# Copies of the weights back to DRAM, spread over four passes by their place in the tile instead of three passes by piece number

## The chip, the cores and the metric

The kernel runs on all 8 cores of one Trainium2 chip. Each core works on its own sequences; the weights are the same for all, and no core waits for another. The metric is the device time of the slowest of the 8 cores in one execution, in microseconds (us). As the slowest of eight is noisy, I also use the mean span of the 8 cores over all fast runs ("mean of the cores").

Some executions fall in a slow state: the cores of one die, sometimes of both, have a lower mean granted TensorE clock (0.81 to 0.97), and the execution takes 2217 to 2540 us. They are left out everywhere, so all medians below are of the fast runs alone.

## The reference, cut to what matters

```python
xn = rmsnorm(x, g_pre_mix)
z  = xn @ w_in                         # xa, ga, u, v, gates: six projections of 1024
# A: conv -> gates -> scan -> * gelu(ga) -> @ w_br_a      (merge piece "ba")
# B: gelu(u) * (w_s @ layernorm(gelu(v)) + b_s) -> @ w_br_b   (merge piece "bb")
mix = (sigmoid(g_a) * o_a + sigmoid(g_b) * o_b) @ w_out   # "ma", "mb", "out"
x = x + rmsnorm(mix)
gate, up = split(rmsnorm(x) @ w_ffn_in)                   # "fg", "fu"
x = x + rmsnorm((silu(gate) * up) @ w_ffn_out)            # "fo": the channel mixer
```

The inputs are float32; the kernel multiplies in bf16.

## The kernel before

A core has nine tiles of at most 512 tokens. The weights are not kept on chip: every tile streams all of them through a ring of 8 slots, in 70 pieces, nearly all of 128 x 2048 elements. The projections have 16 pieces (xa, v, ga, u), the merge 20 (mb, bb, ma, ba, out), the channel mixer 34 (fg, fu, fo).

A piece is first read as f32 from `wall` by a DMA that GpSimd issues and that casts to bf16. In one chosen pass (0 for tile 0, 1 for tile 1 and so on) the bf16 piece is copied back from the ring to a DRAM scratch `wsc`. From then on SyncE loads it as bf16 from there: half the bytes to read.

```python
def PASS_OF(pid):
    return pid % 3

def load(pid):
    slot = free.popleft()
    have[pid].append(slot)
    n = PIECES[pid][2] * PIECES[pid][4]
    if pid in cached:
        dma("sp", ... wring[:, slot, 0:n] <- wsc[pid, :, 0:n] ...)
        return
    dma("pool", ... wring[:, slot, 0:n] <- wall[pid, :, 0:n] ...)
    k = seen.get(pid, 0)
    seen[pid] = k + 1
    if k == PASS_OF(pid):
        todo_wo[slot] = (pid, n)        # to be copied back when it has landed

def copy_back(slot):
    pid, n = todo_wo.pop(slot)
    dma("sp", ... wsc[pid, :, 0:n] <- wring[:, slot, 0:n] ...)
    cached.add(pid)
```

The order of instructions is not written by hand. The work is cut into stages ("v of tile 1, rows 0 to 127", "second norm of tile 0, part 3"). A list scheduler on the host keeps a clock for every engine and for DMA, and always emits the stage that can start earliest, by priority among those ready. A dry run fixes the order in which pieces are streamed; the second run records the program. The DMA clock charges by kilobytes, so it sees f32 loads as twice as long:

```python
DMA_NS, DMA_LAT = 3.3, 2000.0
...
self.dma_free = max(self.dma_free, start) + kb * self.DMA_NS
...
while True:
    fill()                                  # copies and loads that may go now
    best = None
    for e in P.ENGS:
        on = [(offer(q[0]), rank(q[0], n), q) for n, q in streams.items() if ...]
        ...
    if best is None:
        break
    emit(best[1][2].popleft())
...
plan = record(Prog(), None)                 # dry run
P = Prog()
record(P, plan)
```

Of the kernel before, what the change touches and what calls it, by code (L numbers as in the profile page):

```python
# [32 lines left out]
def piece_table():  # L33

    tab = []
    ids = {}

    def add(name, items):
        ids[name] = []
        for it in items:  # L40
            ids[name].append(len(tab))
            tab.append(it)

    add("xa", [("w_in", 0, 8, 256 * h, 256) for h in range(4)])
    add("v", [("w_in", 4 * kh, 4, 3 * D + 512 * n, 512) for n in range(2) for kh in range(2)])
    add("ga", [("w_in", 0, 8, D + 256 * h, 256) for h in range(4)])
    add("u", [("w_in", 0, 8, 2 * D + 256 * h, 256) for h in range(4)])
    add("mb", [("w_in", 0, 8, 5 * D + 256 * h, 256) for h in range(4)])
    add("bb", [("w_br_b", 0, 8, 256 * h, 256) for h in range(4)])
    add("ma", [("w_in", 0, 8, 4 * D + 256 * h, 256) for h in range(4)])  # L50
    add("ba", [("w_br_a", 0, 8, 256 * h, 256) for h in range(4)])
    add("out", [("w_out", 4 * kh, 4, 512 * n, 512) for n in range(2) for kh in range(2)])
    add("fg", [("w_ffn_in", 0, 8, 256 * q, 256) for q in range(NFF // 2)])
    add("fu", [("w_ffn_in", 0, 8, DFF + 256 * q, 256) for q in range(NFF // 2)])
    add("fo", [("w_ffn_out", 4 * r, 4 if r < 5 else 2, 512 * n, 512) for n in range(2) for r in range(6)])
    return tab, ids


PIECES, PID = piece_table()


def PASS_OF(pid):

    return pid % 3
NPIECE = len(PIECES)


class _Op:
# [213 lines left out]
def build_program():  # L282
    nc = bass.Bass("TRN2", target_bir_lowering=False)

    def din(name, shape):
        return nc.dram_tensor(name, list(shape), F32, kind="ExternalInput").ap()
# [7 lines left out]
    sc_in = din("sc", [128, NCH, 2, 3])  # L294
    wall = din("wall", [NPIECE, 128, PSZ])
    vecs_in = din("vecs", [128, NVEC, NCH])
# [12 lines left out]

    wsc = nc.dram_tensor("wsc", [NPIECE, 128, PSZ], BF16).ap()  # L310

# [3 lines left out]
    with contextlib.ExitStack() as es:  # L315
# [79 lines left out]
        def record(P, plan):  # L395
# [71 lines left out]
            cached = set()  # L467
            have = {pid: deque() for pid in range(NPIECE)}
            todo_wo = {}
            wo = deque()  # L470
# [6 lines that stand above are left out]
                    dma("sp", lambda e: e.dma_start(out=wring[:, slot, 0:n], in_=wsc[pid, :, 0:n]), ring_sems[slot], n / 4,  # L477
                        [("wsc", pid)], [("wr", slot)])
                    return
                dma("pool", lambda e: e.dma_start(out=wring[:, slot, 0:n], in_=wall[pid, :, 0:n]), cast_sems[slot], n / 2,  # L480
                    (), [("wr", slot)])
# [3 lines that stand above are left out]
                    todo_wo[slot] = (pid, n)  # L485
# [934 lines left out]
def make_in_maps(inputs):  # L1420
    f = lambda a: np.ascontiguousarray(np.asarray(a, dtype=np.float32))
    g = {k: f(v) for k, v in inputs.items()}
    wall = np.zeros((NPIECE, 128, PSZ), np.float32)
    for i, (name, k0, kc, c0, n) in enumerate(PIECES):
# [39 lines left out]
```

## Time and profile before

| | |
|---|---|
| time, median | 2179.73 us |
| mean of the cores (9 fast runs, on the chip of experiments 1 to 4) | 2170.5 us |
| f32 loads / bf16 loads / copies back | 139 / 491 / 70 |

The page of the slowest core. Part 1 gives busy time and share by engine, part 2 shares in 40 slices of the span (tenths), part 3 the DMA queues (q1: SyncE's plain transfers; q0: GpSimd's casting loads), part 4 the chain of waits that ended last.

```profile
span 2202.9 us, 34614 instructions; the slowest of 8 cores (2163.8 to 2202.9 us)
PE 2086.7 (95%) x10518; PEld 1021.6 (46%) x10666; DVE 1203.0 (55%) x1880; ACT 901.9 (41%) x1536; POOL 380.2 (17%) x761
...
DMA  9698899987778657773545554576575666365663
...
q1 hardware_dynamic: 97362, 341.48, 46.4%
q0 software_dynamic: 20016, 72.36, 20.8%
...
PE 85%; DMA 6%; DVE 3%; issue 3%; ACT 3%; POOL 1%; SPq 0%; DVEq 0%; POOLq 0%; ACTq 0%
```

(148 matmul records of this core are missing from the trace: 10666 weight loads, 10518 matmuls.) PE is the limit, and DMA is close to full (8 or 9 tenths in eight of the first nine slices) only in the first fifth of the span, while most pieces still come as f32. From part 3, 139 f32 loads take 20.8% of 16 engines' 2202.9 us, 3.3 us of all 16 for each; the plain queue takes 1.57 us per 512 KB.

Spans and clocks of four cores:

```profile
core 0: 2169.2 us, clock 0.981
...
core 3: 2163.8 us, clock 0.983
core 4: 2202.9 us, clock 0.970
core 5: 2192.6 us, clock 0.970
```

Cores 4 and 5 of this execution were held at clock 0.81 from about 552 us on, for 142 and 161 us. The other six cores ran the same program without that (0.97 to 1.00 at 560 to 690 us), so I read stages on core 0. Stretches of core 0: each line has the stretch, its length, busy us (and instructions) of PE, PEld, DVE, ACT, POOL, the granted clock, the DMA share, GB/s.

```profile
core 0: us, PE busy (x) PEld busy (x) DVE busy (x) ACT busy (x) POOL busy (x), PEclk, DMA share, GB/s
0.00:250.00 250.00, 198.51 (x908) 91.34 (x909) 167.83 (x250) 148.55 (x224) 72.95 (x146) 0.90 0.86 178
250.00:350.00 100.00, 100.00 (x463) 45.23 (x462) 32.46 (x48) 14.56 (x25) 13.90 (x27) 1.00 0.93 175
425.00:450.00 25.00, 19.15 (x78) 7.90 (x78) 15.62 (x23) 10.32 (x18) 5.70 (x16) 0.86 0.91 256
480.00:550.00 70.00, 62.58 (x312) 29.08 (x311) 58.28 (x89) 44.41 (x67) 17.57 (x38) 0.95 0.77 177
550.00:660.00 110.00, 110.00 (x530) 50.54 (x528) 36.58 (x55) 22.84 (x45) 12.80 (x26) 1.00 0.92 203
```

The matmul count is the number to read. A full 25 us holds some 116 matmuls of 512 columns (0.216 us each); narrower ones take less (8 of 128 columns took 0.45 us on core 0 of before at 396 us), so a full stretch can hold more. At 425 to 450 us there are 78: a hole in tile 1's merge. At 480 to 550 us tile 1 goes from its merge to its channel mixer.

### The profile page before, as it was taken

The numbers are of one execution on the slowest core, as the hardware profiler recorded it, in microseconds if no ns is written. First come the engines' busy times: TensorE is split into PE (matmuls) and PEld (weight loads), VectorE is DVE, ScalarE is ACT, GpSimd is POOL, SyncE is SP. The second block draws the span as 40 slices with busy tenths as digits, with TensorE's granted clock in tenths as the row PEclk, the third lists the DMA queues.
The fourth block names the chain that finished last, engine by engine and source line by source line (L and its number), as shares of the span: only waits on it lengthen the run. The fifth ranks groups of instructions, "written<-read, shape, count | busy, mean of one in ns | idle before, by whom it ended". The sixth has DMA issues, their size and how long they took to land.

```text
span 2202.9 us, 34614 instructions; the slowest of 8 cores (2163.8 to 2202.9 us)
## 1 busy us (share of the span) xinstructions
PE 2086.7 (95%) x10518; PEld 1021.6 (46%) x10666; DVE 1203.0 (55%) x1880; ACT 901.9 (41%) x1536; POOL 380.2 (17%) x761
## 2 busy tenths in 40 slices
PE   4899799998999999999999999999999999899998
PEld 2344344444444444444444444455555645445553
DVE  5757634468322685167833585268357636763342
ACT  3737511465112571147412571266148224722211
POOL 2213212322002220022001210121022012112000
PEclk8899899999888999999999999999999999999999
DMA  9698899987778657773545554576575666365663
GB/s 187 141 196 164 166 185 200 254 202 172 170 178 221 191 188 185 209 240 131 182 149 188 199 191 150 170 246 220 191 256 182 224 188 231 122 201 173 200 203 108
DMA packets 117703, 416.10 MB, mean 189 GB/s; under 512 B 14537, under 2 KB 14545, under 8 KB 117522
## 3 DMA queue, kind: packets, MB, share of 16 engines
q1 hardware_dynamic: 97362, 341.48, 46.4%
q0 software_dynamic: 20016, 72.36, 20.8%
q8 instruction: 90, 1.47, 0.3%
q14 instruction: 91, 0.75, 0.1%
q10 hardware_dynamic: 144, 0.05, 0.0%
HBM read 432.62 MB, written 53.54 MB: 221 GB/s over the span
## 4 chain that ended last, share of the span: by engine, by line
PE 85%; DMA 6%; DVE 3%; issue 3%; ACT 3%; POOL 1%; SPq 0%; DVEq 0%; POOLq 0%; ACTq 0%
PE ps L707 58%; PE ps L1236 13%; PE ps L1140 5%; PE ps L954 5%; DMA wring<-wsc 2%; DMA wring<-wall 2%; DMA xin<-xp 1%; PE ps L659 1%; DVE xcf L830 1%; PE ps L848 1%; PE ps L1249 1%; PE ps L1016 1%; DMA x<-xp 0%; ACT ffT L653 0%; POOL stats L638 0%
## 5 line engine op out<-in xcount | busy, mean ns | idle before, releaser
L707 PE MATMUL ps<-hnT,wring 128*128 128x512 bf16 (+2 forms) x3133 | 637.6, 364 | 8.6 <-DVE hnT L664 4.1
L707 PE MATMUL ps<-xnT,wring 128*128 128x512 bf16 (+2 forms) x2842 | 615.9, 366 | 21.3 <-DMA wring<-wall 7.2
L707 PEld LDWEIGHTS ps<-hnT,wring 128*128 128x128 bf16 x3168 | 311.8, 99 | 325.3 <-issue 56.1
L707 PEld LDWEIGHTS ps<-xnT,wring 128*128 128x128 bf16 x2880 | 281.0, 99 | 303.8 <-issue 59.7
L1236 PE MATMUL ps<-wring,ffT 128*128 128x512 bf16 (+1 forms) x1334 | 303.8, 387 | 3.6 <-DVE hnT L664 1.7
L1215 ACT ACTIVATE sgt<-ps 128x512 f32<-128x512 f32 (+2 forms) x198 | 109.5, 554 | 448.7 <-PE ps L707 419.2
L1219 DVE SCALAR_TENSOR_TENSOR sgt<-sgt,ps 128x512 f32<-128x512 f32 (+2 forms) x198 | 125.4, 633 | 234.9 <-PE ps L707 230.8
L1236 PEld LDWEIGHTS ps<-wring,ffT 128*128 128x128 bf16 (+1 forms) x1364 | 134.5, 99 | 170.6 <-issue 34.6
L830 DVE SCALAR_TENSOR_TENSOR xcf<-xa,vecs_sb,xcf 128x512 f32<-128x512 f32 (+2 forms) x240 | 163.5, 681 | 26.8 <-DVE xcf L830 1.2
L480 POOL DMA_DIRECT2D wring<-wall x139 | 78.9, 568 | 461.9 <-PE ps L707 305.2
L1104 DVE SCALAR_TENSOR_TENSOR ffT<-ffT,ps 128x512 f32<-128x512 f32 (+1 forms) x122 | 76.3, 631 | 149.2 <-PE ps L707 130.0
L1221 DVE SCALAR_TENSOR_TENSOR ffT<-sgt,ps 128x512 bf16<-128x512 f32 (+2 forms) x198 | 125.8, 635 | 46.4 <-PE ps L707 43.0
L1095 ACT ACTIVATE ffT<-ps 128x512 f32<-128x512 f32 (+1 forms) x128 | 69.1, 554 | 164.2 <-PE ps L707 153.3
L707 PE MATMUL ps<-gsT,wring 128*128 128x512 bf16 (+2 forms) x569 | 127.4, 367 | 4.2 <-DVE gsT L1036 2.8
L707 PE MATMUL ps<-hgT,wring 128*128 128x512 bf16 (+2 forms) x568 | 124.8, 363 | 5.5 <-ACT ffT L1095 5.1
L631 POOL TENSOR_SCALAR stats<-stats 128x1 f32<-128x1 f32 (+1 forms) x132 | 34.9, 264 | 539.7 <-ACT ffT L644 442.4
L1140 PE MATMUL ps<-wring,vnm 128*128 128x512 bf16 (+1 forms) x517 | 117.1, 383 | 7.8 <-POOL vnm L1110 3.1
L954 PE MATMUL ps<-wring,xnT 128*128 128x512 bf16 (+1 forms) x513 | 116.1, 379 | 1.6 <-DMA wring<-wsc 0.8
L1259 ACT ACTIVATE sgt<-ps 128x512 f32<-128x512 f32 x66 | 38.5, 594 | 175.1 <-PE ps L1236 159.0
L638 POOL TENSOR_TENSOR stats<-stats,nhalf 128x1 f32<-128x1 f32 x165 | 100.0, 606 | 24.5 <-POOL stats L631 0.5
L1110 POOL TENSOR_TENSOR vnm<-ffT 128x512 bf16<-128x512 f32 (+1 forms) x58 | 69.2, 1194 | 191.5 <-DVE ffT L1104 143.6
L887 DVE TENSOR_TENSOR_SCAN chI<-chA,hst,chI 128x512 f32<-128x512 f32 (+1 forms) x72 | 89.1, 1237 | 7.8 <-DVE chI L886 0.5
(141 smaller groups left out, 1962.6 us busy)
## 6 DMA issues: line engine op xcount, KB each, us to landing
wring<-wsc SPq DMA_DIRECT2D x475, 512.0 KB, 4.6
wring<-wall POOLq DMA_DIRECT2D x137, 512.0 KB, 9.3
wsc<-wring SPq DMA_DIRECT2D x68, 512.0 KB, 8.6
xin<-xp SPq DMA_DIRECT2D x30, 512.0 KB, 7.4
x<-xp SPq DMA_DIRECT2D x29, 512.0 KB, 8.3
yp<-x SPq DMA_DIRECT2D x29, 512.0 KB, 6.9
wring<-wsc SPq DMA_DIRECT2D x16, 256.0 KB, 3.6
yp<-xin SPq DMA_DIRECT2D x4, 256.0 KB, 2.0
```

Source lines behind the costliest of these rows:

```text
L480: dma("pool", lambda e: e.dma_start(out=wring[:, slot, 0:n], in_=wall[pid, :, 0:n]), cast_sems[slot], n / 2, (), [("wr", slot)])
L638: pool(lambda e: e.tensor_tensor(out=stats[0:PT, r2:r2 + 1], in0=stats[0:PT, r:r + 1], in1=nhalf[0:PT, :], op=ALU.pow), 180, [("st", r), ( ...
L707: mm(lambda e, k=k: e.matmul(ps[:, b, 0:nt], lhsT=wv[:, k, m * 128:(m + 1) * 128], rhs=rhsT[:, k, 0:nt], start=(k == 0), stop=(k == NCH - ...
L830: dve(lambda e, k=k, dst=dst, win=win: e.scalar_tensor_tensor(out=dst, in0=win(k), scalar=vecs[:, V_CW + k, c:c + 1], in1=dst, op0=ALU.mul ...
L887: dve(lambda e: e.tensor_tensor_scan(out=chI[:, j, 0:np_], data0=chA[:, j, 0:np_], data1=chI[:, j, 0:np_], initial=hst[:, c:c + 1], op0=AL ...
L954: mm(lambda e, k=k, wv=wv, b=b: e.matmul(ps[0:PT, b, :], lhsT=xnT[:, k, col:col + PT], rhs=wv[:, k % 4, :], start=(k == 0), stop=(k == NCH ...
L1104: dve(lambda e: e.scalar_tensor_tensor(out=ap[:, 0:nt], in0=tsg[i][0][:, 0:nt], scalar=1.0, in1=ps[:, b, 0:nt], op0=ALU.add, op1=ALU.mult) ...
L1140: mm(lambda e, k=k, n=n, wv=wv: e.matmul(ps[0:PT, pr + n, :], lhsT=mixT[:, k, col:col + PT], rhs=wv[:, k % 4, :], start=(k == 0), stop=(k ...
L1215: act(lambda e: e.activation(out=sgt[:, i, 0:nt], in_=ps[:, b, 0:nt], func=AF.Tanh, scale=0.5), nt, [("ps", b)], [("sgt", i)])
L1219: dve(lambda e: e.scalar_tensor_tensor(out=sgt[:, i, 0:nt], in0=sgt[:, i, 0:nt], scalar=1.0, in1=ps[:, bg, 0:nt], op0=ALU.add, op1=ALU.mul ...
L1221: dve(lambda e: e.scalar_tensor_tensor(out=ffT[:, j, 0:nt], in0=sgt[:, i, 0:nt], scalar=0.5, in1=ps[:, bu, 0:nt], op0=ALU.mult, op1=ALU.mu ...
L1236: mm(lambda e, j=j, kk=kk, b=b, PT=PT, col=col: e.matmul(ps[0:PT, b, :], lhsT=ffT[:, j, col:col + PT], rhs=wv[:, kk, :], start=(j == 0), s ...
```

## The change

The intent is to take copies out of the first tile's channel mixer, where DMA is close to full (share 0.93 at 250 to 350 us), and to spread them by what the piece is used for: projections in passes 1 and 2, merge in 1 to 3, channel mixer in 2 to 4 (counted from 1).

```diff
 PIECES, PID = piece_table()
+NPIECE = len(PIECES)
 
 def PASS_OF(pid):
 
-    return pid % 3
-NPIECE = len(PIECES)
+    kind = next(k for k, v in PID.items() if pid in v)
+    i = PID[kind].index(pid)
+    if kind in ("xa", "v", "ga", "u"):
+        return i % 2
+    return i % 3 + (1 if kind in ("fg", "fu", "fo") else 0)
```

## The prediction

> **What bounds it now.** PE. On the page of the slowest core (core 4, 2202.9 us) PE is busy 95% and holds 85% of the chain of waits; DMA holds 6%. Core 4 is slowest by its clock: about 0.8 from 550 to 700 us, where core 3 (2163.8 us) has 1.00. DMA matters early: its share is 0.9 to 1.0 up to 450 us, then 0.4 to 0.8. Most other idle time of PE up to 550 us is startup and dependent work. DMA clearly costs one hole: the chain shows two bf16 loads of 17.7 and 15.3 us at 411-446 us, in tile 1's merge; cores 0, 3, 4 run 78, 83, 89 matmuls at 425-450 instead of 117: 6 to 8 us lost.
>
> **Costs.** By the queue table, 139 f32 loads take 20.8% of 16 engines' span, 3.3 us each; the plain queue takes 46.4% for 341 MB, 1.6 us per 512 KB: a bf16 load or a copy. An f32 load in place of a bf16 one adds 1.7 us. [...]
>
> **What changes.** Counting pieces: f32 loads 139 -> 159 (by pass 70/46/23/0 -> 70/52/27/10); copies 70 (24/23/23/0 -> 18/25/17/10). DMA time +35 us. By place:
> - Tile 0 before its channel mixer, with tile 1's first projections: copies 12 -> 18 of pass 1, +3 of pass 2: +13 us DMA in 0-250 us, where its share is 0.8 to 0.9. Estimate +3 us.
> - Tile 0's channel mixer (250-350 us, DMA 0.95 to 1.0, PE full): 12 copies go, -19 us DMA. The ring enters tile 1 full.
> - Tile 1's v and merge, with tile 2's first projections (350-500): about 8 f32 loads and 5 copies fewer, -22 us DMA. The hole goes: -7 us.
> - Tile 1's channel mixer: f32 loads 22 -> 34, copies 11 -> 12, +22 us DMA where its share is 0.9 (cores 0, 3). Like tile 0's before: saturated, PE full, ring drained at the end. +1 us.
> - Tiles 2 and 3: channel mixers with 22 and 10 f32 loads at shares of 0.7 to 0.8: hidden.
>
> Sum -3 us. The host's list scheduler models DMA too, so instruction order shifts: +-8 us, and more for throttling.
>
> **Predicted: 2177 us, 8 in 10 between 2150 and 2200. Faster by over 2%: 0.03; within 2%: 0.94; slower by over 2%: 0.03.**
>
> **What would show it.** 159 f32 loads, 70 copies; no long bf16-load steps in the chain at 400-450 us, about 117 matmuls per 25 us there on unthrottled cores; DMA share of 250-350 us down to about 0.85, of 550-660 us up to about 1.0 with PE still full; PE waits for f32 loads before 250 us up a few us. The clock's dip to 0.86 beside the hole goes [...].
>
> **What would make it wrong.** Tile 1's channel mixer (about 128 us of DMA against 113 us of matmuls) stalling PE: +10 to 20 us. The first 250 us being tighter than their share says, since copies wait for their f32 load at the head of the queue that also issues bf16 loads (SP waited 227 us so). Or the hole being queue order, not bandwidth, and only moving.

Two passages that no run of this case shows are cut from this text. No term of its sum goes with them: +3 -7 +1 = -3 us stands in full. But its "DMA time +35 us" adds f32 loads, bf16 loads and copies, and that these add up on the same 16 engines was the author's assumption: the page charges both queues to 16 engines (46.4% and 20.8% of their span in the kernel before), and no run tests it.

## More of the kernel before

PE's waits on core 0 from 390 to 620 us (waiting line, releaser: us in total, times, longest):

```profile
PE ps L707 <- DMA wring<-wsc: 5.6, 2, 4.8
PE ps L1016 <- DVE vnm L990: 4.7, 2, 3.3
PE ps L707 <- ACT gvf L967: 1.9, 1, 1.9
```

`wring<-wsc` is a bf16 load (the hole). L1016 is the spatial matmul of tile 2, which waits for the layernorm of v just before it.

## The result, and the profile after

| | before | after |
|---|---|---|
| time, median | 2179.73 us (3 fast of 4 runs) | 2169.02 us (2166.51 to 2171.38, 4 runs) |
| ratio of fast runs | | 0.9947, 95% interval 0.9928 to 0.9967 |
| the same, another chip, 5 rounds | 2181.00 us | 2165.69 us; 0.9923 (0.9901 to 0.9945) |
| mean of the cores, that other chip | 2170.5 us | 2153.2 us |

A ratio is the mean time of one kernel's fast runs over that of the other's fast runs of the same rounds, so it is not quite the ratio of the medians. The gain is clear of noise and below 2%.

The page of the slowest core after:

```profile
span 2169.8 us, 34771 instructions; the slowest of 8 cores (2141.6 to 2169.8 us)
PE 2068.7 (95%) x10666; PEld 1014.1 (47%) x10666; DVE 1204.7 (56%) x1880; ACT 902.4 (42%) x1537; POOL 393.2 (18%) x781
...
DMA  8799798877999498855776454656575676365563
...
q1 hardware_dynamic: 94482, 332.56, 46.2%
q0 software_dynamic: 22896, 81.27, 23.4%
...
PE 83%; DMA 7%; DVE 4%; issue 2%; ACT 2%; POOL 1%; DVEq 0%; POOLq 0%; SPq 0%; ACTq 0%
```

The same four cores after, none at a low clock for long:

```profile
core 0: 2145.6 us, clock 0.988
...
core 3: 2163.9 us, clock 0.986
core 4: 2141.6 us, clock 0.987
core 5: 2151.8 us, clock 0.988
```

There are now 159 f32 loads, 471 bf16 loads and still 70 copies. DMA works more, not less: the two queues' shares times the span are 1480 us before and 1510 us after. Yet the program is faster. The same stretches of core 0 after:

```profile
core 0: us, PE busy (x) PEld busy (x) DVE busy (x) ACT busy (x) POOL busy (x), PEclk, DMA share, GB/s
0.00:250.00 250.00, 202.68 (x942) 92.49 (x943) 165.25 (x241) 151.32 (x228) 70.69 (x143) 0.93 0.87 190
250.00:350.00 100.00, 95.50 (x467) 43.97 (x465) 55.41 (x86) 19.59 (x33) 19.61 (x40) 1.00 0.90 156
425.00:450.00 25.00, 23.48 (x109) 10.40 (x108) 22.30 (x32) 18.79 (x30) 6.85 (x15) 1.00 0.88 211
480.00:550.00 70.00, 70.00 (x373) 33.67 (x372) 58.08 (x87) 38.52 (x59) 18.52 (x37) 1.00 0.90 191
550.00:660.00 110.00, 110.00 (x535) 50.86 (x534) 39.90 (x55) 25.89 (x49) 20.26 (x39) 1.00 0.99 219
```

The hole at 425 us is nearly gone (78 to 109 matmuls). But the largest step is at 480 to 550 us: 312 to 373. Of PE's waits on core 0 from 390 to 620 us one line is left:

```profile
PE ps L711 <- DMA wring<-wsc: 1.5, 1, 1.5
```

(All lines moved down by 4; L711 was L707.) The layernorm wait of tile 2 is gone, although copies do not touch it. The reason is the order: the order of matmuls on PE differs from that of before in many places, from tile 0's v on. In the changed kernel tile 1's v runs at about 234 to 274 us, from the end of tile 0's merge into the first matmuls of its channel mixer; before, it came at about 345 to 359 us, after that mixer's gate and up matmuls. So the change did two things at once, and the trace alone cannot say which counts.

**A measure of lost PE time.** On a core whose trace has all 10666 matmul records, each record can be matched with its stage, since the program's order is known. I take the start-to-start time of successive matmuls beyond 0.216 us (or beyond the shortest seen at that place on any core, where that is less), and sum it by the tile of the later matmul. Below are means over the complete cores, in us; before is without core 5, which was at clock 0.81. The rest of the time is the same work at full clock; the 11 us before the first matmul are not counted.

| | tile 0 and startup | tile 1 | tile 2 | tiles 3 to 8 | sum |
|---|---|---|---|---|---|
| before | 59.6 | 9.1 | 16.7 | 42.9 | 128.4 |
| after (the run after_again below) | 54.3 | 13.8 | 4.6 | 40.8 | 113.4 |

The sum falls by 15.0 us, the mean of the cores by 17.3 us. All but some 2 us of it is in tiles 0 to 2. As a yardstick of noise: the first profile of the changed kernel, on the other chip, gives 54.9 / 12.4 / 4.4 / 42.8, sum 114.5. So two profiles of one program differ by up to 2 us in a column, and a difference of that size is not to be relied on.

### The profile page after: what moved, and what is told of

It is laid out like the page before. It is cut to its first block, busy times and chain, and to the rows that moved or that the text cites. A ratio compares the mean times of both kernels' runs of the same rounds, so it can differ in the third digit from the quotient of the medians.

```text
span 2169.8 us, 34771 instructions; the slowest of 8 cores (2141.6 to 2169.8 us)
## 1 busy us (share of the span) xinstructions
PE 2068.7 (95%) x10666; PEld 1014.1 (47%) x10666; DVE 1204.7 (56%) x1880; ACT 902.4 (42%) x1537; POOL 393.2 (18%) x781
## 4 chain that ended last, share of the span: by engine, by line
PE 83%; DMA 7%; DVE 4%; issue 2%; ACT 2%; POOL 1%; DVEq 0%; POOLq 0%; SPq 0%; ACTq 0%
PE ps L711 56%; PE ps L1240 13%; PE ps L1144 5%; DMA wring<-wall 4%; PE ps L958 4%; DMA xin<-xp 2%; DVE xcf L834 1%; PE ps L663 1%; PE ps L852 1%; PE ps L1253 1%; PE ps L1020 1%; ACT ffT L657 0%; POOL stats L642 0%; DVE ffT L1108 0%; DVE xcf L830 0%
## 5 line engine op out<-in xcount | busy, mean ns | idle before, releaser
L711 PE MATMUL ps<-hnT,wring 128*128 128x512 bf16 (+2 forms) x3168 | 628.5, 359 | 8.3 <-DMA wring<-wall 6.0
L711 PE MATMUL ps<-xnT,wring 128*128 128x512 bf16 (+2 forms) x2880 | 610.5, 363 | 16.0 <-DMA wring<-wall 8.6
L711 PEld LDWEIGHTS ps<-hnT,wring 128*128 128x128 bf16 x3168 | 308.2, 98 | 317.8 <-issue 16.4
L711 PEld LDWEIGHTS ps<-xnT,wring 128*128 128x128 bf16 x2880 | 279.2, 99 | 294.6 <-issue 39.5
L1240 PE MATMUL ps<-wring,ffT 128*128 128x512 bf16 (+1 forms) x1364 | 297.4, 379 | 1.7 <-DVE hnT L668 1.5
L484 POOL DMA_DIRECT2D wring<-wall x159 | 89.3, 563 | 495.7 <-PE ps L711 357.7
L711 PE MATMUL ps<-hgT,wring 128*128 128x512 bf16 (+2 forms) x576 | 125.6, 362 | 6.9 <-ACT ffT L1099 6.7
L711 PE MATMUL ps<-gsT,wring 128*128 128x512 bf16 (+2 forms) x576 | 125.3, 362 | 3.9 <-DVE gsT L1040 2.9
L958 PE MATMUL ps<-wring,xnT 128*128 128x512 bf16 (+1 forms) x528 | 121.3, 385 | 6.2 <-DMA wring<-wall 5.7
L1271 DVE TENSOR_TENSOR gvf<-ps,gbc_pf 128x512 f32<-128x512 f32 (+1 forms) x33 | 20.6, 684 | 145.5 <-ACT sgt L1263 145.5
```

The costliest lines, as they stand in the source:

```text
L484: dma("pool", lambda e: e.dma_start(out=wring[:, slot, 0:n], in_=wall[pid, :, 0:n]), cast_sems[slot], n / 2, (), [("wr", slot)])
L711: mm(lambda e, k=k: e.matmul(ps[:, b, 0:nt], lhsT=wv[:, k, m * 128:(m + 1) * 128], rhs=rhsT[:, k, 0:nt], start=(k == 0), stop=(k == NCH - ...
L958: mm(lambda e, k=k, wv=wv, b=b: e.matmul(ps[0:PT, b, :], lhsT=xnT[:, k, col:col + PT], rhs=wv[:, k % 4, :], start=(k == 0), stop=(k == NCH ...
L1240: mm(lambda e, j=j, kk=kk, b=b, PT=PT, col=col: e.matmul(ps[0:PT, b, :], lhsT=ffT[:, j, col:col + PT], rhs=wv[:, kk, :], start=(j == 0), s ...
```

## The experiments

Theory "copies": the time comes from the moved DMA work, as predicted. Theory "order": it comes from the other order that the scheduler settles on. To part them, the scheduler first plans under one rule, then its order of stages and its choice of PSUM banks (the buffers that matmuls write) are replayed while copies and loads follow another rule. The order in which pieces are streamed into the ring stays that of the plan, so here it counts as part of the order. The core of that edit, cut:

```diff
-        def record(P, plan):
+        def record(P, plan, pass_of, forced=None):
...
-                if k == PASS_OF(pid):
+                if k == pass_of(pid):
...
+            for key in forced[0] if forced else ():
+                fill()
+                assert home[key][0].key == key
+                emit(home[key].popleft())
-            while True:
+            while not forced:
...
-        plan = record(Prog(), None)
+        plan = record(Prog(), None, ORDER_PASS)[0]
+        _, order, picks = record(Prog(), plan, ORDER_PASS)
         P = Prog()
-        record(P, plan)
+        record(P, plan, COPY_PASS, (order, picks))
```

With both rules alike the replay gives the program of before, and that of after, stage for stage on every engine. All twelve runs gave correct results; each call had 5 rounds with the kernel before on the same chip.

### 1. old_order_new_copies

`ORDER_PASS = by_number` (pid % 3), `COPY_PASS = by_place` (the change).

> The order of stages on every compute engine and the choice of PSUM banks are those of the kernel before (planned with the old rule and then replayed); only the passes in which pieces are copied back, and so which loads are f32 or bf16, are those of the change. Theory 'order' (the 12 us come from the different order that the host's planner settled on): within 4 us of before, about 2177 to 2185 us, and PE still loses matmuls at 480 to 550 us (about 310 instead of 325 or more per 70 us on undisturbed cores). Theory 'copies' (the 12 us come from the lighter DMA load at 350 to 500 us, as predicted): about 2170 us, ratio 0.995 or below, and at 425 to 450 us about 117 matmuls per core instead of about 80.

Measured: 2188.64 us median, ratio 1.003 (1.0011 to 1.0048); mean of the cores 2174.9 against 2170.5 us. The new copies alone make the kernel slower. Stretches of core 0, columns as above, and its longest PE wait from 390 to 620 us (L1044 was L1016):

```profile
425.00:450.00 25.00, 24.39 (x114) 10.78 (x112) 16.80 (x25) 12.65 (x23) 6.04 (x15) 1.00 1.02 272
480.00:550.00 70.00, 61.62 (x301) 28.44 (x299) 56.90 (x86) 42.70 (x65) 19.09 (x38) 0.95 0.64 156
```

```profile
PE ps L1044 <- DVE vnm L1018: 5.5, 2, 4.0
```

The hole is gone (114 matmuls), as theory "copies" said, and the gap at 480 to 550 us stays (301), as theory "order" said. Both mechanisms are real. Its lost time is 67.6 / 9.4 / 13.1 us in tiles 0, 1, 2: a cost of 8.0 us in tile 0 outweighs a gain of 3.3 in tiles 1 and 2.

### 2. new_order_old_copies

The reverse.

> The reverse: order of stages and PSUM banks are those of the changed kernel, the passes of the copies those of before (pid % 3; 139 f32 loads). Theory 'order': keeps most of the gain, 2168 to 2173 us, with 350 or more matmuls at 480 to 550 us. Theory 'copies': loses it, about 2181 us, ratio 1.00, with a hole of 6 to 8 us again in tile 1's merge at 400 to 450 us.

Measured: 2176.97 us median, ratio 0.9994 (0.9969 to 1.0019); mean of the cores 2162.5 us, 8.0 below before. So the slowest core shows no clear gain, the mean of the cores does. The same stretches of core 0, and below them its longest PE waits from 390 to 620 us (lines moved down by 28: L735 was L707, L1168 was L1140):

```profile
425.00:450.00 25.00, 19.82 (x77) 8.13 (x76) 12.77 (x19) 8.91 (x16) 5.14 (x16) 0.84 1.02 269
480.00:550.00 70.00, 62.64 (x299) 28.42 (x300) 51.25 (x77) 44.64 (x68) 15.64 (x32) 0.95 0.73 188
```

```profile
PE ps L735 <- DMA wring<-wsc: 5.2, 1, 5.2
PE ps L1168 <- DMA wring<-wall: 4.8, 2, 3.4
PE ps L735 <- DMA wring<-wall: 1.7, 1, 1.7
```

The hole is back (77). And at 480 to 550 us the new order is no better than the old one (299): the layernorm wait is gone, but PE now waits there for f32 loads (`wring<-wall`), which the old copies still ask for. My expectation of 350 or more matmuls was a miss. Of these four kernels only the one with both changes fills this stretch: 312 before, 301 and 299 with one change, 373 with both. As such a count also depends on how many narrow matmuls fall into the stretch, here is the lost time between 480 and 550 us too, mean of the complete cores: 10.0 us before, 9.7 and 7.3 with one change, 1.0 with both (after_again).

### 3. number_plus_one

```diff
-    return pid % 3
+    return (pid + 1) % 3
```

> The kernel before with (pid + 1) % 3 in place of pid % 3, planned freely: as many copies in each pass but for one, DMA work equal to one f32 load, another arrangement. Theory 'order' (the planner's result moves by several us with any change of the rule): away from before by 4 us or more in either direction. Theory 'copies': within 3 us of before, since the DMA work by stage is the same.

Measured: 2192.06 us, ratio 1.0033 (0.9999 to 1.0066); mean of the cores 2172.9 against 2170.5 us. The ratio is not clear of noise. By the mean of the cores kernel and before differ by 2.4 us, which is within the 3 us of theory "copies", by the medians by 11 us, which is theory "order"; so the time decides nothing. Below the surface the order did move: lost time is 48.4 / 25.9 / 14.0 us in tiles 0, 1, 2 against 59.6 / 9.1 / 16.7 before. Shifts of over 10 us per tile came out nearly even.

### 4. after_again

The changed kernel once more, beside the three above.

> The changed kernel itself again, on the same chip as the three others and interleaved with the kernel before: ratio 0.994 to 0.996 under either theory. If it is nearer to 1, the gain is smaller than first measured.

Measured: 2165.69 us, ratio 0.9923; mean of the cores 2153.2 us. The four corners, by the mean of the cores, all from one chip:

| | old copies | new copies | effect of the copies |
|---|---|---|---|
| old order | 2170.5 | 2174.9 | +4.4 |
| new order | 2162.5 | 2153.2 | -9.3 |
| effect of the order | -8.0 | -21.7 | |

The gain of 17.3 us is not a sum of two parts. The new copies pay only in an order that suits them.

### 5 and 6. new_order_mixer_moved, new_order_rest_moved

New order; only the channel mixer's copies by place (172 f32 loads), or only those of projections and merge (126). Against the replay with both rules by place:

```diff
-COPY_PASS = by_place
+COPY_PASS = mixer_by_place      # fg, fu, fo by place, the others pid % 3
...
-COPY_PASS = by_place
+COPY_PASS = rest_by_place       # fg, fu, fo pid % 3, the others by place
```

> Order of stages and banks of the changed kernel, replayed; only the channel mixer's copies go by place (passes 2 to 4), projections and merge by number as before; 172 f32 loads. The gap to close is the 1.3 per cent between the new order with old copies (mean of all cores 2162.5 us) and the changed kernel (2153.2 us). If what helps is that tile 0's channel mixer no longer copies back, this closes most of it: mean of the cores 2151 to 2156 us, ratio 0.992 to 0.995, and tile 0 before its channel mixer loses no more than with the old copies. If what helps is the fewer f32 loads of projections and merge in pass 2, it stays at 2160 to 2165 us, ratio 0.998 to 1.001, with PE waiting for bf16 loads again at 425 to 455 us.

> The complement: order of the changed kernel, only projections and merge by place, the channel mixer by number; 126 f32 loads, 30 copies in pass 1. If the relief of tile 0's channel mixer is what helps: mean of the cores 2160 to 2168 us, ratio 0.998 to 1.003, since tile 0 has the extra copies and the mixer keeps its own. If the lighter pass 2 of projections and merge is what helps: 2153 to 2157 us, ratio 0.993 to 0.996.

Measured: mixer moved 2168.62 us, ratio 0.9936 (0.991 to 0.9961), mean of the cores 2157.4, between the two ranges that I had named; rest moved 2164.71 us, ratio 0.9915 (0.989 to 0.9941), mean 2152.6. The kernel before, on that chip: mean 2170.2. Emptying the first channel mixer of copies gives about half of what the copies are worth (5.1 of 9.3 us by the mean of the cores); the fewer f32 loads of projections and merge give all of it, with the mixer's copies left where they were. The mixer's part of the change adds nothing on top (2153.2 for all, in run 4).

### 7 and 8. after_v_late, before_v_early

Is tile 1's v, moved in front of tile 0's channel mixer, the piece of the order that matters? One more constraint for the scheduler, in each direction:

```diff
 # changed kernel: tile 1's v waits for the last gate and up matmuls of tile 0
-after=[("xte", t, s)] + ...
+after=[("xte", t, s)] + ([("fin", 0, NFF - 1)] if t == 1 else []) + ...
 # kernel before: tile 0's channel mixer waits for tile 1's v
-after=[("hte", t, ns - 1)] + ...
+after=[("hte", t, ns - 1)] + ([("v", 1, 3)] if t == 0 and j == 0 else []) + ...
```

> The changed kernel, planned freely, but tile 1's projection v must come after the last gate and up matmuls of tile 0's channel mixer, about where it stood in the kernel before. If v's place in front of the channel mixer (where the new order has it fill the wait for tile 0's second norm) is what the order is worth: tile 0's wait for its transposes comes back, some 10 us at 225 to 250 us, and the mean of the cores rises by 5 us or more to 2158 us or above, ratio 0.996 or above. If other parts of the order are worth more: below 2156 us, ratio up to 0.994.

> The reverse on the kernel before: tile 1's v is forced ahead of tile 0's channel mixer, the rest planned freely, copies by number. If v's place is the cause: tile 0's wait for the second norm shrinks from 10 us to under 4 us and the mean of the cores falls from 2170 to 2163 us or below, ratio 0.997 or below. The planner's own model says the opposite (slower), since the rest of the order moves too; if that holds: ratio 1.00 or above, and v's place alone is not the cause.

Measured: v late 2164.14 us, ratio 0.9917 (0.9889 to 0.9946), mean of the cores 2152.9, as fast as the changed kernel. v early 2192.49 us, ratio 1.0033 (1.0002 to 1.0064), mean 2178.6, slower than before. This piece of the order is not the cause; for v early the scheduler's own clock had said so in advance. The wait for tile 0's second norm does follow v (5.1 us with v late, none in the changed kernel, 4.4 with v early, 10.5 before), but the time comes back elsewhere: v late loses 57.4 / 9.0 / 5.6 us in tiles 0, 1, 2, v early 48.9 / 38.2 / 8.1.

### 9. before_v2_early

The kernel before, with the layernorm wait of tile 2 attacked directly:

```diff
-after=[("hte", t, ns - 1)] + ...
+after=[("hte", t, ns - 1)] + ([("v", 2, 3)] if t == 1 and j == 2 else []) + ...
```

> The kernel before, copies by number, with one more rule for the planner: tile 2's v must be done before the third gate matmul group of tile 1's channel mixer. Up to 500 us the order is unchanged. In the kernel before, the spatial matmuls of tile 2 come straight after the last of v and wait 3.3 and 1.4 us for its layernorm (5.0 us lost at tile 2's sp, mean of the complete cores). If that piece of the order is what the new order saves at 480 to 560 us: the loss at tile 2's sp falls under 1 us and the mean of the cores falls by 4 to 6 us, ratio 0.997 to 0.998. If the loss only moves to the next stage: within 2 us of before.

Measured: 2184.62 us, ratio 0.997 (0.9919 to 1.002), inconclusive by time. On the chip of runs 9 to 12 five of the nine fast runs of before were disturbed (means of the cores of 2175.6 to 2180.0, the others 2169.0 to 2170.8), so I compare with 2170: this kernel's mean is 2170.2. PE waits of core 1 from 480 to 620 us:

```profile
PE ps L707 <- DMA wring<-wall: 4.9, 1, 4.9
PE ps L707 <- ACT gvf L967: 1.9, 1, 1.9
PE ps L659 <- ACT ffT L653: 0.8, 2, 0.4
```

The loss at tile 2's spatial stage fell from 5.0 to 0.1 us, and one of 4.9 us for an f32 load took its place on core 1. Tile 2 as a whole loses 9.7 us (16.7 before), tile 1 loses 17.0 (9.1 before). The loss moved; this is the second part of what I had expected.

### 10 and 11. new_order_proj_moved, new_order_merge_moved

New order; only the projections' copies by place (132 f32 loads), or only the merge's (133), all others by number.

> Order of the changed kernel, replayed; only the projections' copies by place, merge and channel mixer by number; 132 f32 loads. Copies of pass 1 rise by 2, f32 loads of projections in pass 2 fall from 10 to 8, in pass 3 from 5 to 0. Of the 10 us (mean of the cores, 2162.5 against 2152.6) that projections and merge are worth together, the projections' share is estimated at 4 to 6 us: 2157 to 2159 us, ratio 0.994 to 0.996.

> The same with only the merge's copies by place; 133 f32 loads. Copies of pass 1 rise by 4, f32 loads of the merge in pass 2 fall from 14 to 10. If the merge's f32 loads make the hole in tile 1's merge, this takes the larger part: 2153 to 2157 us, and the loss at 425 to 455 us falls from 5.6 to about 2 us. Tile 0 before its channel mixer loses 4 to 6 us more than with the old copies (42 us).

Measured, by the mean of the cores: 2157.4 (projections; 2175.34 us median, ratio 0.9929, 0.9885 to 0.9973) and 2153.4 (merge; 2166.65 us, ratio 0.9894, 0.9833 to 0.9954). The ratios share the disturbed runs of before and look too good. Lost time with the new order and different copies:

| copies by place | tile 0 | tile 1 | tile 2 | tiles 0 to 2 |
|---|---|---|---|---|
| none (new_order_old_copies) | 50.0 | 26.7 | 7.7 | 84.4 |
| projections | 56.0 | 18.0 | 1.4 | 75.4 |
| merge | 50.3 | 20.2 | 6.9 | 77.4 |
| channel mixer | 49.6 | 19.0 | 5.9 | 74.5 |
| projections and merge | 55.9 | 13.2 | 3.1 | 72.2 |
| all (after_again) | 54.3 | 13.8 | 4.6 | 72.7 |

Each part alone saves 7 to 10 us, two or three together only 12, which suggests that they relieve the same backlog of the ring in tiles 1 and 2. The order of the rows is not to be read: in tiles 3 to 8, where little differs, these six profiles lose 37.5 to 43.5 us, and by the mean of the cores the merge's copies alone (2153.4) beat the projections' alone (2157.4). Nor does the stretch at 480 to 550 us decide the time. On core 1 the projections' copies fill it and the merge's do not, first line and second:

```profile
480.00:550.00 70.00, 70.00 (x367) 33.48 (x366) 58.23 (x88) 41.32 (x63) 16.96 (x33) 1.00 0.73 183
480.00:550.00 70.00, 65.78 (x327) 30.20 (x326) 53.89 (x82) 42.08 (x65) 18.68 (x36) 0.98 0.72 178
```

The guess about the merge's loads and the hole was wrong: with the merge moved, the loss at tile 2's first projection, where the hole sits in this order, is still 5.3 us (5.6 with none moved); with the projections moved it is 0.0, but 6.0 us appear in tile 1's merge. The extra cost in tile 0 comes with the projections' copies (50 to 56 us), not with the merge's (50.3), though I had expected it of the merge's.

### 12. v_late_rest_moved

The version that the runs pointed to: order planned by the new rule with v late, replayed with projections and merge by place and the mixer by number (126 f32 loads).

> The best version that the runs so far point to: the order planned by the new rule with tile 1's v held behind tile 0's channel mixer (tiles 0 to 2 lost 66 us there against 67 in the changed kernel, with less in tile 1), replayed with the lighter copies (projections and merge by place, channel mixer by number, 126 f32 loads). If the two add up: mean of the cores 2149 to 2152 us, ratio 0.990. If v late needs the ring that the moved mixer copies leave: slower than the changed kernel, ratio 0.994 or above.

Measured: 2164.47 us (2162.5 to 2172.36), ratio 0.9891 (0.9851 to 0.9931) against a disturbed before; mean of the cores 2150.8 us, 2.4 below the changed kernel's 2153.2 on another chip. Lost time is 57.8 / 9.1 / 3.0 us. The mean is in the range expected if the two add up. But the two kernels were never run side by side: the changed kernel has means of 2153.5 and 2153.2 us on its two chips, and the undisturbed runs of before have 2170.0 to 2170.5 on three. So a small gain is likely and not shown.

## Why the prediction was right or wrong

- **The time.** Predicted 2177 us (2150 to 2200, within 2% at 0.94); measured 2169.02, and 2165.69 on another chip. Range and class are right. The sum of -3 us was too small: -11 and -15 us by the medians. That its sign came out right was luck: in the order that the sum took as given, the same copies cost 4.4 us (run 1).
- **PE-bound, and DMA-limited only early: right.** PE stays at 95%, and all but some 2 us of the saved PE idle time lies in tiles 0 to 2.
- **Counts: right.** 159 f32 loads, 70 copies, HBM reads up by 8.9 MB, DMA time up by 30 us (predicted 35).
- **"The hole goes: -7 us": right, isolated by run 1.** With the old order and the new copies, 78 matmuls at 425 to 450 us become 114, and the losses of tile 2's two stages around the hole fall from 8.2 to 2.2 us, so -6.0. The sign I had named for it was wrong in one point: a bf16 load of 15 us still stands in the chain of waits at 423 to 438 us after the change, but PE waits only 1.5 us for it. A long transfer in the chain is not a long wait. As predicted, the clock at 425 to 450 us rises from 0.86 to 1.00: before, core 0 was granted clock 0.50 for 6.8 us from 442.2 us on, 2.3 us into its wait of 4.8 us for a load. The dip went with the hole on core 0 of all four kernels: 0.86 and 0.84 where the hole is (before, run 2), 1.00 and 1.00 where it is gone or nearly so (run 1, after).
- **"Tile 0: +3 us": right in sign, too small.** Lost time in tile 0 rises by 8.0 us in the old order and by 4.3 in the new one. The sign named for it came, larger than "a few us": PE's waits for f32 loads before 250 us rise from 5.3 to 14.5 us on core 0. I took the DMA share of 0.86 for free room. But that is an average: in run 1, 6.6 us of the cost stand at tile 0's v (0.1 before), where PE of core 0 waits 3.8 us for an f32 load; the DMA share there is 0.93 at 60 to 80 us and 0.31 at 80 to 100 us (0.83 and 0.34 before). That copies hold this load up is likely, not shown.
- **"Tile 1's channel mixer saturated, PE full: +1 us": right.** DMA share 0.92 to 0.99, PE busy 110.00 of 110 us both times.
- **DMA share of 250 to 350 us "down to about 0.85": right for the copies** (0.93 to 0.80 in run 1), but 0.90 in the changed kernel, where the new order puts tile 1's v there.
- **"Instruction order shifts: +-8 us": the step that failed.** I took the order for noise, centred on zero and independent of the copies. It is neither: in the new order the kernel is 8.0 us faster with old copies and 21.7 us faster with new ones, by the mean of the cores (with old copies the slowest core shows no clear gain, ratio 0.9994). The copies' own effect, which I put at -3, is +4.4 in the old order and -9.3 in the new. A likely reason, not tested: the scheduler charges f32 loads twice and chooses an order in which that DMA load can be borne, so rule and order belong together.
- **What stays open.** Which stages of the order carry the gain. Two candidates were tried (tile 1's v, tile 2's v), and both only moved the loss. Shown is the place where the two meet: at 480 to 550 us PE is full only with the new order (which removes the layernorm wait) and the new copies (those of the projections are enough there; they remove the waits for f32 loads). Even that place is not the whole gain: with only the merge's copies moved it is not full, and the mean of the cores is as good (2153.4). That the planner's tie of rule and order explains all 17 us is argued, not shown.

All 159 f32 loads of the changed kernel are in GpSimd's queue and all 471 bf16 loads in SyncE's. Whether the casting loads could be issued elsewhere was not tested.

## What to carry to other kernels

When a host-side scheduler models the resource you change, a change of data movement is also a change of instruction order: budget the order as an effect of its own, and separate the two by replaying one order with the other's transfers. What several waits cost need not add up: removing one of them, or half of the load, may gain all there is (projections and merge alone reached a mean of the cores of 2152.6 us, all copies 2153.2), and removing a wait alone may only hand it to the next (run 9: the loss at tile 2's spatial stage fell from 5.0 to 0.1 us, one of 4.9 us for an f32 load came on core 1). Count matmuls per stretch rather than trust the shares of the chain: a long transfer in the chain need not cost PE much (here PE waited 1.5 us for one of 15 us).

## What the runs show of clock and DMA

- In the fast runs all 8 cores ran dense matmuls (PE busy 95% on both pages) at a mean clock of 0.97 to 0.99. In the profile of before only cores 4 and 5 of their die fell to 0.81, at 552 us, for 142 and 161 us; cores 6 and 7 did not (0.97 at 560 to 690 us). In the slow run of after_again (2524.23 us) cores 0 to 3 had 0.820 to 0.825 and cores 4 to 7 0.985 to 0.987.
- An f32-to-bf16 load of 128 x 2048 elements took 3.3 us of all 16 engines and a plain bf16 load or copy 1.57 us. That is in line with the bytes read (1 MB against 512 KB), not with those written; no run separates the effect of the cast from that of the queue.
- A DMA share of 0.86 over 250 us did not mean free room: about 13 us of extra transfers (the prediction's estimate, counted by pieces at 3.3 and 1.6 us each) went with 8.0 us more lost PE time in tile 0 in the old order, and 4.3 us more in the new one, where the share was 0.88.
